# The norms' sums of squares take a PSUM slot of the bank pool instead of the aux pool

## The chip, the cores and the metric

The kernel runs on one core of a Trainium2 chip. The metric is the device time of one execution in microseconds, the median of several runs. Profiles are taken from one profiled execution; their times are counted from the start of its span. PE is TensorE, DVE is VectorE, ACT is ScalarE, and SP's queue issues most of the transfers.

## The reference

The reference is the trunk of a diffusion model over 512 latent tokens (SEQ) and 256 context tokens (CTX), with a model width of 1024. There are two layers. Each has a half-step SwiGLU, a token mixer and another half-step SwiGLU; the mixer is a bidirectional S5 state space model in layer 0 and a bidirectional gated linear attention (GLA) with four heads in layer 1. Cut to what matters here:

```python
def rmsnorm(x, w):
    xf = x.astype(F32)
    y = xf * lax.rsqrt(jnp.mean(xf * xf, axis=-1, keepdims=True) + NORM_EPS)
    return (y * w.astype(F32)).astype(x.dtype)

def ffn_half_step(x, w_norm, shift, scale, gate, w_in, w_out):
    h = rmsnorm(x, w_norm) * (1.0 + scale) + shift
    return x + 0.5 * gate * swiglu_ffn(h, w_in, w_out)

for i in range(DEPTH):
    mod_x = (jnp.einsum('bd,de->be', jax.nn.silu(c), ada_w[i]) + ada_b[i])[:, None, :]
    ...
    x = ffn_half_step(x, ...)
    hx = rmsnorm(x, norm_w[i, 1]) * (1.0 + sx[4]) + sx[3]
    # S5 in layer 0, GLA in layer 1
    x = x + sx[5] * yx
    x = ffn_half_step(x, ...)
return rmsnorm(x, final_norm_w)
```

Every step begins with an RMS norm over the width, with a shift, a scale and a gate that are products of the conditioning vector with large matrices. In the GLA each head's output goes through a norm of its own (over 256 values) before a gate and the output product.

## The kernel before

The stream `xT` is held transposed: 8 tiles of 128 channels on the partitions, 768 tokens along the free axis. So the sum of squares of a token runs over the partitions, and PE forms it. `squares` (L142) squares the 8 tiles on ACT (L147, L150) and adds them up on DVE (L151). `rstd` (L154) then multiplies each stretch of 128 tokens of that sum by a column of ones (L163), which puts the sums of 128 tokens on the partitions, in one column of a PSUM tile for each stretch. DVE L167 is the only reader of that tile. Three Newton steps on DVE (L169 to L175) make the reciprocal root `y` of it, and `spread` (L178, matmul L182) broadcasts `y` back over the partitions into a PSUM tile, which the norm's multiplications (L201) read. ACT L218 and DVE L219 split the normed operand `h` into a high and a low part.

All large products are made of three passes (`mm3`, L113 to L115): weight high times operand high, weight high times operand low, weight low times operand high. ACT L88 and DVE L89 split each weight.

PSUM has one pool with two tags of tiles of 128 partitions by 512 floats: `bank` with 6 slots (products, modulation blocks, spreads, the transposes of the start and of the end, the GLA's V tiles and outputs) and `aux` with 2 slots (the sums of L163, the columns of a modulation block at L406, small transposes, the level products, transposes and states of the GLA heads, and small steps of the S5 stage).

`rstd` is called 22 times: twice at the start (halves of the tokens), three times each for the norm ahead of S5, for the norm behind it and for the two norms between the half-steps of layers 0 and 1 and ahead of the GLA (thirds of the tokens), four times in the GLA (once a head, with two parts of 4 stretches each), twice for the norm behind the GLA, and twice at the end. In the norms the call stands in a queue of work that `tick` counts down: `norm` puts the sum some steps after the squares, and the spread three steps after the sum.

A modulation block (L399 to L406) is 16 matmuls of the conditioning vectors with a quarter of the weights into one `bank` tile; ACT L403 copies it (`adar`), four matmuls L406 bring it into columns in an `aux` tile, and DVE L446 adds the bias. At the start four such blocks follow the two sums in the program.

In the GLA the work of one head is: products of queries and keys level by level (`level`, L1210 to L1244, `aux` tiles), decays (`decays`, L1259 to L1268), transposes and states (L1287 to L1304, `aux` tiles), outputs (two `bank` tiles, matmuls L1320 to L1322, squares `gsq` on ACT L1324 and gating on DVE L1326), the gates of the next head, and then `rstd`. The squares `gsq` and the tile `geb` of decay factors (in the levels at L1231) share the two slots of one tag in SBUF. The spread of that sum and the normalised output (`normed`, which makes `goh` and `gol`) come some levels into the next head. Between these steps `fill` takes projections of the next heads (V tiles by L1109 to L1111, keys and queries by `mm3` from `h`) and output products of the head before (`goh`, `gol`) out of lists that are written by hand (`ORDER`, `COUNTS`).

At the end the last half-step SwiGLU does its last products for two halves of 256 tokens. After each half `final` scales `xT` by the norm weight (L1576), makes the squares and the sum, transposes the result in four `bank` tiles (L1583) and multiplies by `y` (L1586, L1588). So the program has the first half's products, its sum, its transposes, and only then the second half's products.

The order of instructions on each engine is not that of the program alone. The framework plans a timeline of its own, in which the program's order is the priority: work that stands later in the program is moved ahead into time that the plan shows as idle. The tiles of a tag are allocated as the program runs.

Of the kernel before, what the change touches and what calls it, by code (L numbers as in the profile page):

```python
# [38 lines left out]
class Core:  # L39
# [114 lines left out]
    def rstd(self, parts, count=D, scale=1.0):  # L154


        nc = self.nc
        n = parts[0].shape[-1]
        nt = n // P
        b = self.aux()  # L160
        for t in range(nt):
            for i, part in enumerate(parts):
                nc.tensor.matmul(b[:, t:t + 1], part[:, t * P:(t + 1) * P], self.ones[:, 0:1],  # L163
                                 start=(i == 0), stop=(i == len(parts) - 1))
        v, y, z = (self.tmp.tile([P, 4], F32, tag=f"rs{i}", name="rs", bufs=2)[:, :nt] for i in range(3))
        i32 = mybir.dt.int32
        nc.vector.tensor_scalar(out=v, in0=b[:, :nt], scalar1=1.0 / (count * scale * scale),  # L167
                                scalar2=EPS / (scale * scale), op0=ALU.mult, op1=ALU.add)
        nc.vector.tensor_scalar(out=y.bitcast(i32), in0=v.bitcast(i32), scalar1=-0.5, scalar2=1597463007.0,  # L169
                                op0=ALU.mult, op1=ALU.add)  # L170
        nc.vector.tensor_scalar(out=v, in0=v, scalar1=-0.5, scalar2=None, op0=ALU.mult)  # L171
        for _ in range(3):
            nc.vector.tensor_mul(z, y, y)  # L173
            nc.vector.tensor_mul(z, z, v)  # L174
            nc.vector.scalar_tensor_tensor(out=y, in0=z, scalar=1.5, in1=y, op0=ALU.add, op1=ALU.mult)  # L175
        return y
# [1438 lines left out]
```

## Time and profile before

| | us |
|---|---|
| median of 3 runs | 2891.98 |
| lowest and highest run | 2890.7 and 2893.82 |
| profiled execution, its own time | 2892.6 |
| its span | 2890.8 |
| PE busy | 2734.3 (95%) |
| DVE busy | 1795.5 (62%) |
| ACT busy | 856.8 (30%) |

The mean granted clock of PE in that execution was 0.967 of full speed. Rows of the timeline have the start, the duration, the engine, the line, the operation, the tile written and the tiles read, the shapes and a count where several instructions are put together; in square brackets stands the idle time of the engine before it and what ended it. Groups of lines have the count, then the busy time and the mean duration in nanoseconds. Matmuls are pipelined, so that the durations of neighbours overlap, and sums of them can be more than the time they take together.

### The profile page before, as it was taken

How to read it: one execution, taken by the hardware profiler on the slowest of the kernel's cores; microseconds unless marked ns; L12 is line 12 of the kernel's file. 1: busy time of each engine (PE TensorE's matmuls, PEld its weight loads, DVE VectorE, ACT ScalarE, POOL GpSimd, SP SyncE). 2: the span in 40 equal slices, each digit the busy share in tenths (PEclk: the TensorE clock that was granted, in tenths of full speed). 3: DMA queues.
4: the chain of work that ended last, by engine and by line, in shares of the span. 5: the costliest groups of instructions: out<-in, count | busy, mean ns of one | idle time of the engine just before them, and what ended most of it. 6: DMA issues, size and time to landing. Idle time of an engine off the chain costs nothing. (4 is left out here: it accounts for less than half of the span.)

```text
span 2890.8 us, 44937 instructions
## 1 busy us (share of the span) xinstructions
PE 2734.3 (95%) x18231; PEld 2579.4 (89%) x18231; DVE 1795.5 (62%) x4080; ACT 856.8 (30%) x1386; POOL 22.3 (1%) x57
## 2 busy tenths in 40 slices
PE   7999999996559999999999999999999899799998
PEld 5899999995459999999999999999988798688887
DVE  6699999436894565557427555665268687643433
ACT  4222222224362421122123221121236453332223
POOL 0000000000020000000000000000000000000000
PEclk9999999997779999999999999999999899899999
DMA  6545554516653133334321333333103112233330
GB/s 225 162 115 154 150 161 137 173 65 198 220 149 99 59 96 102 95 111 121 91 59 45 110 106 106 101 104 95 54 23 88 44 45 74 66 116 91 94 93 30
DMA packets 396044, 305.43 MB, mean 106 GB/s; under 512 B 57994, under 2 KB 344188, under 8 KB 395836
## 3 DMA queue, kind: packets, MB, share of 16 engines
q1 hardware_dynamic: 391228, 293.12, 34.6%
q10 hardware_dynamic: 4608, 9.44, 0.9%
q8 instruction: 143, 2.34, 0.3%
q14 instruction: 65, 0.53, 0.1%
HBM read 275.77 MB, written 30.41 MB: 106 GB/s over the span
## 5 line engine op out<-in xcount | busy, mean ns | idle before, releaser
L113 PE MATMUL bank<-h,whi 128*128 128x384 f32 (+3 forms) x3160 | 1044.0, 333 | 8.6 <-ACT whi L88 6.1
L114 PE MATMUL bank<-h,whi 128*128 128x384 f32 (+3 forms) x3160 | 1049.1, 332 | 0.2 <-DVE h L219 0.2
L115 PE MATMUL bank<-h,wlo 128*128 128x384 f32 (+3 forms) x3160 | 1046.9, 332 | 0.0
L113 PEld LDWEIGHTS bank<-h,whi 128*128 128x128 f32 (+1 forms) x3160 | 593.5, 189 | 30.3 <-ACT whi L88 6.7
L88 ACT CAST whi<-wraw 128x1024 fp32r<-128x1024 f32 x313 | 327.3, 1048 | 982.0 <-PE bank L114 930.0
L114 PEld LDWEIGHTS bank<-h,whi 128*128 128x128 f32 (+1 forms) x3160 | 595.6, 189 | 17.7 <-DVE h L219 0.5
L115 PEld LDWEIGHTS bank<-h,wlo 128*128 128x128 f32 (+1 forms) x3160 | 594.3, 188 | 17.6 <-issue 0.6
L89 DVE TENSOR_TENSOR wlo<-wraw,whi 128x1024 fp32r<-128x1024 f32 x313 | 380.5, 1219 | 243.5 <-ACT whi L88 240.0
L114 PE MATMUL bank<-ml,whi 128*128 128x384 f32 (+2 forms) x1360 | 448.0, 330 | 0.0
L113 PE MATMUL bank<-mh,whi 128*128 128x384 f32 (+2 forms) x1360 | 446.0, 331 | 2.1 <-DVE xT L279 1.2
L115 PE MATMUL bank<-mh,wlo 128*128 128x384 f32 (+2 forms) x1360 | 446.0, 329 | 0.0
L279 DVE SCALAR_TENSOR_TENSOR xT<-bank,hg,xT 128x256 f32<-128x256 f32 (+2 forms) x488 | 220.7, 499 | 198.0 <-PE bank L115 197.6
L264 DVE TENSOR_TENSOR sg<-sg,bank 128x384 f32<-128x384 f32 (+2 forms) x166 | 89.4, 539 | 352.8 <-PE bank L115 338.2
L113 PEld LDWEIGHTS bank<-mh,whi 128*128 128x128 f32 x1360 | 256.4, 189 | 9.5 <-DVE xT L279 1.5
L114 PEld LDWEIGHTS bank<-ml,whi 128*128 128x128 f32 x1360 | 257.0, 189 | 6.4 <-issue 0.4
L115 PEld LDWEIGHTS bank<-mh,wlo 128*128 128x128 f32 x1360 | 256.5, 189 | 6.3 <-issue 0.2
L427 DVE SCALAR_TENSOR_TENSOR adaacc<-wraw,cs,adaacc 128x512 f32<-128x512 f32 x336 | 236.9, 744 | 19.1 <-DMA wraw<-in_ada_w_dram 18.6
L265 ACT CAST mh<-sg 128x384 fp32r<-128x384 f32 (+2 forms) x166 | 83.5, 503 | 312.5 <-DVE sg L264 311.5
L263 ACT ACTIVATE sg<-bank 128x384 f32<-128x384 f32 (+2 forms) x166 | 79.5, 479 | 198.5 <-PE bank L115 198.4
L266 DVE TENSOR_TENSOR ml<-sg,mh 128x384 fp32r<-128x384 f32 (+2 forms) x166 | 89.7, 541 | 24.2 <-ACT mh L265 24.1
L150 ACT ACTIVATE sq<-xT 128x256 f32<-128x256 f32 (+1 forms) x126 | 52.1, 428 | 58.7 <-DVE xT L279 39.5
L201 DVE SCALAR_TENSOR_TENSOR nt<-xT,sc,bank 128x256 f32<-128x256 f32 (+2 forms) x136 | 61.6, 474 | 11.5 <-PE bank L182 8.5
(298 smaller groups left out, 2337.0 us busy)
## 6 DMA issues: line engine op xcount, KB each, us to landing
wraw<-in_ffn_w_in_dram SPq DMA_DIRECT2D x176, 512.0 KB, 4.0
wraw<-in_ada_w_dram SPq DMA_DIRECT2D x111, 512.0 KB, 3.8
wraw<-in_ffn_w_out_dram SPq DMA_DIRECT2D x88, 512.0 KB, 3.4
wraw<-in_gla_w_in_dram SPq DMA_DIRECT2D x24, 512.0 KB, 4.0
s5R<-s5r ACTq DMA_DIRECT2D x16, 512.0 KB, 2.8
s5O<-s5g SPq DMA_DIRECT2D x64, 128.0 KB, 2.7
wraw<-in_s_w_glu_dram SPq DMA_DIRECT2D x16, 512.0 KB, 6.1
big<-in_ada_w_dram SPq DMA_DIRECT2D x12, 512.0 KB, 8.8
```

The source lines that it names most:

```text
L88: nc.scalar.copy(out=hi[:, :n], in_=raw[:, :n])
L89: nc.vector.tensor_tensor(out=lo[:, :n], in0=raw[:, :n], in1=hi[:, :n].bitcast(F32), op=ALU.subtract)
L113: mm(out, wh, a[0], start=first, stop=False)
L114: mm(out, wh, a[1], start=False, stop=False)
L115: mm(out, wl, a[0], start=False, stop=last)
L201: nc.vector.scalar_tensor_tensor(out=t[:, a - s:z - s], in0=self.xT[:, k, a:z], scalar=sc[i][:, k:k + 1], in1=r[:, a - s:z - s], op0=ALU.m ...
L263: nc.scalar.activation(sg, banks[0][:, :e - s], AF.Silu)
L264: nc.vector.tensor_mul(sg, sg, banks[1][:, :e - s])
L265: nc.scalar.copy(out=mh[:, o], in_=sg)
L266: nc.vector.tensor_tensor(out=ml[:, o], in0=sg, in1=mh[:, o].bitcast(F32), op=ALU.subtract)
L279: nc.vector.scalar_tensor_tensor(out=self.xT[:, d, a:z], in0=banks[d][:, a - s:z - s], scalar=gate[i][:, d:d + 1], in1=self.xT[:, d, a:z], ...
L427: nc.vector.scalar_tensor_tensor(out=acc[:, v], in0=w[:, k], scalar=col, in1=acc[:, v], op0=ALU.mult, op1=ALU.add)
```

## The change

The PSUM tile into which `rstd` forms its sums is taken from the six slots of `bank` and not from the two slots of `aux`. The instructions and their operands stay as they are; the 22 calls all go this way.

```diff
         nc = self.nc
         n = parts[0].shape[-1]
         nt = n // P
-        b = self.aux()
+        b = self.bank()
         for t in range(nt):
             for i, part in enumerate(parts):
                 nc.tensor.matmul(b[:, t:t + 1], part[:, t * P:(t + 1) * P], self.ones[:, 0:1],
```

## The prediction

> **What bounds the kernel now.** I read first the busy times of the engines, then the windows of single stages, then the timeline around each matmul of L163.
>
> ```profile
> span 2890.8 us, 44937 instructions
> ...
> PE 2734.3 (95%) x18231; PEld 2579.4 (89%) x18231; DVE 1795.5 (62%) x4080; ACT 856.8 (30%) x1386; POOL 22.3 (1%) x57
> ```
>
> ```profile
> 2250.00:2270.00 20.00, 12.30 (x57) 10.95 (x58) 19.88 (x60) 6.91 (x11) 0.10 (x1) 0.61 0.00 1
> 2270.00:2369.75 99.75, 99.75 (x597) 86.70 (x596) 71.44 (x147) 46.16 (x79) 0.51 (x3) 0.99 0.23 64
> 2530.00:2865.00 335.00, 335.00 (x1587) 277.03 (x1586) 130.63 (x157) 88.00 (x115) 0.00 (x0) 1.00 0.29 85
> ```
>
> The columns of a window are its length, then the busy time of PE, weight load, DVE, ACT and POOL, the granted clock, the DMA share and GB/s. PE is the bound, and in the long product stages it is never idle. An idle microsecond that the change makes ahead of such a stage is lost, one that it closes is won. Only the short stages between (here GLA head 0, where DVE is busy for 19.88 of 20 us) can hide anything.
>
> **The change part by part.** No instruction is added or removed: 140 matmuls of L163 write, and 22 instructions of L167 read, a slot of another tag.
>
> ```profile
> L163 PE MATMUL aux<-ones,ssq x76: 164/250/353, 30.0 to 2881.1; 128*128 128x1 f32 x76
> ...
> L167 DVE TENSOR_SCALAR rs<-aux x22: 146/152/163, 31.0 to 2881.4; 128x2 f32<-128x2 f32 x16, 128x4 f32<-128x4 f32 x4, 128x3 f32<-128x3 f32 x2
> ```
>
> So all of the cost is in the order. I take it that the slots of one tag are given out in program order, while the planner moves other work far ahead. Three places speak for it:
>
> ```profile
> 2212.84 0.58 ACT L403 COPY adar<-bank 128x512 f32<-128x512 f32 x1
> ...
> 2241.80 0.28 PE L163 MATMUL aux<-ones,gsq 128*128 128x1 f32 x2
> ...
> 2241.95 1.03 PE L406 MATMUL aux<-quarter,adar 128*128 128x2 f32 x8
> ...
> 2255.36 2.05 PE L1242 MATMUL aux<-gqc,gkc 128*128 128x128 f32 x8 [2.98 <-DVE gqc L1239]
> ...
> 2269.99 1.71 PE L182 MATMUL bank<-ident,rs 128*128 128x128 f32 x8
> ...
> 2271.45 0.36 PE L1109 MATMUL bank<-whi,h 128*128 128x256 f32 x1
> ```
>
> The input of L406 was ready at 2213.42, but its aux tile stands behind that of the sum in the program, and it ran directly after the sum's first matmul, 28.5 us later. In the same way V tile 5 (L1109) ran directly after the spread (L182) whose bank slot stands ahead of it, though PE stood idle for 2.98 us before. The third place is the start, below. With a bank slot, every later product that the planner has hoisted past a sum must wait for that sum's first matmul, and so for its squares; later aux tiles no longer do.
>
> *Start.* The second half's sum holds back the modulation blocks (L399):
>
> ```profile
> 22.50:34.70 12.20, 8.73 (x52) 1.84 (x52) 1.00 1.05 386
> ```
> ```profile
> 33.88 0.56 DVE L151 TENSOR_TENSOR ssq<-ssq,sq 128x384 f32<-128x384 f32 x1
> 34.73 0.83 PE L163 MATMUL aux<-ones,ssq 128*128 128x1 f32 x6
> ...
> 35.42 1.66 PE L406 MATMUL aux<-quarter,adar 128*128 128x2 f32 x8
> ...
> 47.04 0.16 DVE L446 TENSOR_TENSOR mod<-aux,cols 128x8 f32<-128x8 f32 x1
> ```
> ```profile
> 36.00:49.00 13.00, 13.00 (x48) 7.97 (x47) 6.89 (x23) 5.17 (x7) 0.00 (x0) 0.50 0.87 231
> ```
>
> 52 matmuls of L399, 8.73 us, lie before the second sum, and some 12 groups of four have to follow it. The sum itself cannot come before 34.44, where DVE ends. In exchange L406 and the block copies no longer wait. Before, the last shift came at 47.04 on a PE of half clock. After: 34.7, 12 groups of 0.43 us (full clock, 8.73/52 less overlap) to 0.85 us, and three turns through L406 of 1.0 to 1.7 us give 42.9 to 50.0. That is -4 to +3; I take +0.5, near the middle.
> The trace shows that a PE which was idle is granted 0.50. The Trainium skill (TensorE: Matmul & The Clock Gate, Part 1: The HAM clock gate) says that the array works at half clock until about 3.4 us of activity, so that blocks that now start after a wait would start slow; by that alone this term would be an estimated +2 in place of +0.5. The trace agrees as far as its 0.50 goes, but shows 13 us of it rather than 3.4.
>
> *Norms of the FFN halves and the S5 stage.*
>
> ```profile
> 1558.59 0.98 PE L163 MATMUL aux<-ones,ssq 128*128 128x1 f32 x4 [2.34 <-DVE ssq L151]
> ...
> 2126.61 0.58 PE L163 MATMUL aux<-ones,ssq 128*128 128x1 f32 x4 [2.48 <-DVE ssq L151]
> ```
> ```profile
> 670.00:675.00 5.00, 0.99 (x89) 0.77 (x75) 2.62 (x11) 3.59 (x7) 0.00 (x0) 0.89 0.96 295
> ```
>
> These two sums lie in idle gaps of PE and would move into busy PE or delay it: 0.5 us each (0.98 and 0.58 busy), +1.0 (0 to +2). The sums before the S5 stage move by some product groups, but there PE is busy for 0.99 of 5 us and DMA for 0.96: covered, 0; without that cover it would be the 0.6 us of a sum.
>
> *GLA head 0.* The V projection of head 1 was hoisted ahead of head 0's sum:
>
> ```profile
> L1109 PE MATMUL bank<-whi,h 128*128 128x256 f32 x32 | 9.8, 307 | 0.0
> ...
> L1302 PE MATMUL aux<-gv,gkt 128*128 128x256 f32 x8 | 2.8, 442 | 0.0
> L1296 PE MATMUL aux<-gv,gkt 128*128 128x256 f32 x4 | 1.0, 378 | 0.0
> L1287 PE MATMUL aux<-ident,gkb 128*128 128x128 f32 x5 | 0.9, 272 | 0.0
> ```
> ```profile
> 2237.00:2250.00 13.00, 11.37 (x100) 11.09 (x98) 5.73 (x18) 4.35 (x10) 0.00 (x0) 1.00 0.01 1
> ```
> ```profile
> 2247.12 0.43 DVE L1231 TENSOR_TENSOR geb<-gcb 128x256 f32<-128x256 f32 x1 [2.61 <-PE aux L163]
> ```
>
> The lines are those of 2222.5 to 2237.2; L1110 and L1111 have 32 each too. 14.7 us less 4.7 of the other three leaves 10.0 us of moved products. They now start after the sum. Transposes, states and outputs no longer share PE with them and end earlier, by some 5 to 8 us (half to most of the 10). With them the sum comes earlier, and so does geb, which waited 2.61 us for it and starts the levels of head 1. The moved products then fill the idle time of the levels: 1.63 us (2237 to 2250) and 7.70 (2250 to 2270), 9.3 in all. I reckon an idle 3.1 before the sum (10.0 less a chain 6.9 shorter) and 4.5 left in the levels, 7.6: -2. Ends: all of the wait stays (+3 when the levels' gaps take 7 of the 10), or the sum moves by the full 8 (-5).
>
> *Heads 1 to 3.*
>
> ```profile
> L113 PE MATMUL bank<-goh,whi 128*128 128x512 f32 x16 | 6.5, 407 | 0.0
> ...
> L113 PE MATMUL bank<-h,whi 128*128 128x384 f32 x16 | 5.6, 353 | 0.0
> ...
> L1174 PE MATMUL bank<-glow,gwg 32*128 32x384 f32 x1 | 0.5, 481 | 0.0
> ```
> ```profile
> 2369.75:2392.50 22.75, 22.75 (x114) 20.20 (x114) 18.94 (x39) 13.72 (x25) 0.00 (x0) 1.00 0.10 27
> ```
> ```profile
> 2241.58 0.39 PE L1322 MATMUL bank<-gqb,xT 128*128 128x128 f32 x2
> ...
> 2398.41 0.28 PE L163 MATMUL aux<-ones,gsq 128*128 128x1 f32 x2
> ```
>
> Head 2 is the worst place: K of head 3 and the output product of head 1 (16 matmuls each in L113, L114 and L115, 96 of the window's 114) lay ahead of its sum. The other 18 have some 4.6 us, so 18.2 us are moved. The chain of head 2 before its sum (transposes, states, outputs) then has PE to itself. If PE alone paced it, the sum would come 18.2 us earlier, at 2380.2. From 2369.75 to there PE has the 4.6 us and some 3 of outputs (24 matmuls like the L1322 pair, by 0.39 a pair at most 4.7, and pairs overlap), so 10.4 less 7.6, some 3 us idle, of which the planner may fill a part with work that stands earlier in the program: +2.5 (0 to +11; the upper end where the chain doesn't speed up). All that follows is full PE, so it is lost. Head 1's sum has next to nothing hoisted past it, and nothing stands behind head 3's: 0 and 0; without that it would be head 2's price again.
>
> *End of GLA.*
>
> ```profile
> 2501.37 0.99 PE L163 MATMUL aux<-ones,ssq 128*128 128x1 f32 x4 [11.63 <-DVE rs L173]
> ```
>
> This sum ran after 11.63 us of idle PE directly ahead of the spread. The planner may place it elsewhere: -0.4 (-1 to +2).
>
> *Final norm.*
>
> ```profile
> 2865.00 1.47 PE L1583 MATMUL bank<-ident,fy 128*128 128x128 f32 x12
> ...
> 2866.23 0.36 PE L113 MATMUL bank<-mh,whi 128*128 128x256 f32 x1
> ...
> 2866.91 0.42 DVE L151 TENSOR_TENSOR ssq<-ssq,sq 128x256 f32<-128x256 f32 x1 [0.28 <-ACT sq L150]
> ...
> 2869.62 0.50 PE L163 MATMUL aux<-ones,ssq 128*128 128x1 f32 x4
> ```
> ```profile
> 2880.74 0.62 PE aux L163 x4
> ```
>
> The first half's squares end at 2867.33. Until now transposes (L1583) and the second half's products filled PE meanwhile, and L163 came at 2869.62. All of them stand behind that sum in the program; now PE is idle from 2865.0 to about 2867.4: +2.2 (1.5 to 3). In the tail the last transposes come after the sum at 2880.74 and run beside the Newton steps on DVE: 0 (at most +0.3).
>
> **Sum:** 0.5 + 1.0 - 2 + 2.5 - 0.4 + 2.2 = +3.8. The profiled execution took 2892.6 us (its span 2890.8 and 1.8 around it), 0.6 over the median 2892.0. 2892.6 + 3.8 = 2896.4; less 0.6, 2895.8.
>
> **The rivals.** *Slower: head 2 waits.* One mechanism: the transposes and states of head 2 are paced by DVE (18.94 busy of 22.75 us) and not by PE, so the chain hardly speeds up and up to 18.2 us of products have nothing ahead of them. It decides once the first sum comes after about 2386: from there idle grows one for one, to +11 by 2389. With 8 to 11 in place of 2.5: 2901 to 2904. For it speaks the busy DVE; against it that much of that DVE work is weight splitting and gates of head 3 that can stand back.
> *Faster: head 0 closes.* All of the 10 us fit into the 9.3 us of gaps and the levels start 8 us earlier: -8 in place of -2, 2889.8, and with the start at its low end (-4) 2885. Against it: DVE is busy for 19.88 of 20 us in those levels, so they can't get shorter, only earlier.
> *The slots aren't given out in program order* but to whoever comes first in the plan. Then nothing is blocked, and six slots are enough: 2892.0. The three places above speak against it.
>
> **How the numbers follow.** About 0.2%, 5.8 us, is what a measurement of this kernel can tell from no change: under 2886.2 is faster, over 2897.8 slower. The likeliest case (chance 0.52, own range 2889 to 2900) puts 0.15 of its chance over 2897.8, 0.34 within and 0.03 below, since the planner lays the whole order anew and the ends of the terms add to some 6 us each way. Head 2 waits: 0.21, all slower. Head 0 closes: 0.15, 0.12 of it faster. No order: 0.12, all within. Together faster 0.15, within 0.49, slower 0.36. The range runs from 2886.5, the faster case, to 2905, the end of the slower one.
>
> **What would show it.** In the profile after: the first L163 of head 2 before about 2383 with L113 goh behind it (right), or later than 2386 (the slower rival); V tiles of head 1 behind the first L163 of head 0, and geb no longer waiting for it; L399 of the start after the second sum; an idle PE of about 2.2 us near 2865 ended by DVE L151. Products that stand behind a sum in the program and still run ahead of it would refute the rule of order, and with it the whole working; so would a changed busy time of PE.

## The result, and the profile after

The changed kernel takes 2917.86 us (2917.47 to 2918.34 in 4 runs), the kernel before beside it 2891.34 (2889.96 to 2893.82). The ratio is 1.0092, with a 95% interval of 1.0081 to 1.0104: 26.5 us slower. Forecast were 2895.8 us, in a range of 2886.5 to 2905, with "no change" as the likeliest outcome. The time lies 13 us beyond the range, on the side of the slower rival.

First the head of the page of the profile after.

```profile
span 2915.7 us, 44943 instructions
...
PE 2742.7 (94%) x18231; PEld 2585.3 (89%) x18231; DVE 1799.0 (62%) x4080; ACT 859.5 (29%) x1386; POOL 22.3 (1%) x57
```

The span is 24.9 us longer. The same 18231 matmuls kept PE busy for 8.4 us more (2742.7 against 2734.3), so they were slower; the other 16.5 us are idle time. For the place I take the same instruction in both traces and subtract its start before from its start after. This lag is flat for hundreds of microseconds in the product stages and steps up at a few places:

| stretch (time before) | growth of the lag, us | forecast, us |
|---|---|---|
| start, to 650 | +3.3 | +0.5 |
| S5 stage, to 970 | -4.0 | 0 |
| norm behind the S5 stage, 970 to 1020 | +4.6 | not priced |
| norm ahead of layer 1, 1555 to 1600 | +1.6 | +0.5 |
| norm ahead of the GLA, to 2123 | 0.0 | +0.5 |
| GLA and the norm behind it, 2123 to 2505 | +15.8 | +0.1 |
| into the last half-step, to 2860 | +0.4 | 0 |
| last norm and tail | +3.2 | +2.2 |

The first two rows cancel, and are not to be read as an effect: in runs whose code is that of the kernel before up to 970 us, the lag there lay between -6.0 and +1.3 us. So what is left is the GLA, the norm behind the S5 stage, the end, and a smaller step at the norm ahead of layer 1.

For the GLA, windows between the same events (the last sum ahead of it and the first product of the half-step behind it), the kernel before first. After the length come the busy time of PE, the granted clock, the DMA share and GB/s.

```profile
2123.08:2504.53 381.45, 346.70 (x2194) 0.93 0.23 64
```
```profile
2128.55:2525.84 397.29, 354.38 (x2191) 0.91 0.20 59
```

It is 15.8 us longer: 8.2 us more idle PE (42.9 against 34.7) and 7.7 us more busy time for the same work, at a lower clock. In these windows PE was busy for 47.4 us at a granted clock of 0.50, against 32.5 before. So half of the loss there is not a wait but matmuls at half clock in and behind the waits.

The timeline of PE ahead of head 1's sum, before and after the change:

```profile
2310.64 0.34 PE L113 MATMUL bank<-h,whi 128*128 128x384 f32 x1
2310.81 0.38 PE L1322 MATMUL bank<-gqb,xT 128*128 128x128 f32 x2
```
```profile
2308.66 0.70 PE L1302 MATMUL aux<-gv,gkt 128*128 128x256 f32 x2 [0.33 <-ACT xT L1298]
2311.16 0.97 PE L1302 MATMUL aux<-gv,gkt 128*128 128x256 f32 x2 [1.80 <-DVE xT L1304]
2316.05 0.80 PE L1322 MATMUL bank<-gqb,xT 128*128 128x128 f32 x2 [3.92 <-DVE xT L1304]
2316.64 0.64 PE L1320 MATMUL bank<-gs,gv 128*128 128x128 f32 x2
...
2323.07 0.39 PE L1322 MATMUL bank<-gqb,xT 128*128 128x128 f32 x2
2323.30 0.28 PE L163 MATMUL bank<-ones,gsq 128*128 128x1 f32 x2
```

Before, 25 products of `h` (2306.36 to 2310.64) stand between the last state matmuls and the outputs, and PE doesn't wait. After, 24 such products have run already, from 2302.57 to 2308.66, ahead of the last states; the next ones start right behind the L163 (2323.30). So nothing is left between these rows: PE waits for DVE's state updates (L1304), and the output matmuls then take 0.64 us a pair, later 0.39. At head 2 no product at all runs between 2371.66 and the sum; these rows are the end of it:

```profile
2393.38 0.80 PE L1322 MATMUL bank<-gqb,xT 128*128 128x128 f32 x2 [3.67 <-DVE xT L1304]
...
2399.56 0.28 PE L163 MATMUL bank<-ones,gsq 128*128 128x1 f32 x2
```

What DVE did meanwhile is in its own timeline after the change:

```profile
2310.63 0.47 DVE L1304 SCALAR_TENSOR_TENSOR xT<-xT,gtot,aux 128x256 f32<-128x256 f32 x1
2311.02 0.42 DVE L1194 TENSOR_TENSOR_SCAN gcb<-glg,gz 128x128 f32<-128x128 f32 x1
2311.36 0.67 DVE L1194 TENSOR_TENSOR_SCAN gxc<-glg,gz 128x256 f32<-128x256 f32 x1
...
2313.99 1.05 DVE L1194 TENSOR_TENSOR_SCAN gcb<-glg,gz 128x128 f32<-128x128 f32 x3
2314.96 1.04 DVE L1304 SCALAR_TENSOR_TENSOR xT<-xT,gtot,aux 128x256 f32<-128x256 f32 x2
```

Between two state updates of head 1 it works through the scans (L1194) of the gates of head 2, and from 2311.94 to 2313.99 through what these set free in head 2's first levels and decays. This order is the plan's; `gates` of the next head are called ahead of the sum in the program.

The norm behind the S5 stage. Before, PE never waited here; after, the second third's spread comes late:

```profile
993.40 0.50 PE L163 MATMUL bank<-ones,ssq 128*128 128x1 f32 x4
...
1002.87 0.68 PE L182 MATMUL bank<-ident,rs 128*128 128x128 f32 x4 [3.11 <-DVE rs L175]
```
```profile
982.69 0.50 PE L163 MATMUL aux<-ones,ssq 128*128 128x1 f32 x4
...
999.22 0.60 PE L182 MATMUL bank<-ident,rs 128*128 128x128 f32 x4
```

The sum itself (second fence: before) moved by 10.7 us. From it to the spread stand the Newton steps, which DVE fits in among its other work in 8.8 us, and the spread waits for the last of them. Behind the wait the granted clock is 0.50 from 1004.2 to 1007.6 us, so that 3.11 us of idle time cost 4.6.

The end has an idle PE ahead of either sum, as forecast for the first, ended by DVE L151:

```profile
2889.08 0.61 PE L163 MATMUL bank<-ones,ssq 128*128 128x1 f32 x4 [2.23 <-DVE ssq L151]
...
2905.23 0.92 PE L163 MATMUL bank<-ones,ssq 128*128 128x1 f32 x4 [2.23 <-DVE ssq L151]
2906.00 3.29 PE L1583 MATMUL bank<-ident,fy 128*128 128x128 f32 x16
```
```profile
2878.70 1.91 PE L1583 MATMUL bank<-ident,fy 128*128 128x128 f32 x16
2880.74 0.61 PE L163 MATMUL aux<-ones,ssq 128*128 128x1 f32 x4
```

In the tail the 16 transposes moved from ahead of the sum (second fence: before) to behind it, and take 3.29 us where they took 1.91; the granted clock is 0.50 from 2905.4 to 2908.8 us.

### The profile page after: what moved, and what is told of

Its sections match the earlier page's. It is cut to its first block, busy times and chain, and to the rows that moved or that the text cites. A ratio compares the mean times of both kernels' runs of the same rounds, so it can differ in the third digit from the quotient of the medians.

```text
span 2915.7 us, 44943 instructions
## 1 busy us (share of the span) xinstructions
PE 2742.7 (94%) x18231; PEld 2585.3 (89%) x18231; DVE 1799.0 (62%) x4080; ACT 859.5 (29%) x1386; POOL 22.3 (1%) x57
## 5 line engine op out<-in xcount | busy, mean ns | idle before, releaser
L113 PE MATMUL bank<-h,whi 128*128 128x384 f32 (+3 forms) x3160 | 1042.4, 333 | 15.5 <-ACT h L218 9.4
L114 PE MATMUL bank<-h,whi 128*128 128x384 f32 (+2 forms) x3160 | 1048.0, 333 | 0.3 <-DVE h L219 0.3
L115 PE MATMUL bank<-h,wlo 128*128 128x384 f32 (+2 forms) x3160 | 1045.7, 332 | 0.0
L113 PEld LDWEIGHTS bank<-h,whi 128*128 128x128 f32 (+1 forms) x3160 | 593.1, 189 | 37.1 <-ACT h L218 10.3
L114 PEld LDWEIGHTS bank<-h,whi 128*128 128x128 f32 x3160 | 595.6, 189 | 17.9 <-DVE h L219 0.6
L115 PEld LDWEIGHTS bank<-h,wlo 128*128 128x128 f32 x3160 | 594.3, 188 | 17.7 <-issue 0.6
L201 DVE SCALAR_TENSOR_TENSOR nt<-xT,sc,bank 128x256 f32<-128x256 f32 (+2 forms) x136 | 62.3, 477 | 20.5 <-PE bank L182 16.6
```

The lines of the kernel that those rows point to most:

```text
L113: mm(out, wh, a[0], start=first, stop=False)
L114: mm(out, wh, a[1], start=False, stop=False)
L115: mm(out, wl, a[0], start=False, stop=last)
L201: nc.vector.scalar_tensor_tensor(out=t[:, a - s:z - s], in0=self.xT[:, k, a:z], scalar=sc[i][:, k:k + 1], in1=r[:, a - s:z - s], op0=ALU.m ...
```

## The experiments

In most of the kernels `rstd` counts its calls and takes a bank slot for some of them only:

```diff
     def rstd(self, parts, count=D, scale=1.0):
+        self.nr = getattr(self, 'nr', -1) + 1
...
-        b = self.bank()
+        b = self.bank() if self.nr in (14, 15, 16, 17) else self.aux()
```

Calls 0 and 1 are the start, 2 to 4 the norm ahead of S5, 5 to 7 the norm behind it, 8 to 13 the two norms between the half-steps and ahead of the GLA, 14 to 17 the GLA heads, 18 and 19 the norm behind the GLA, 20 and 21 the last norm. "Growth in the GLA" is the lag at 2600 less the lag at 2000 us of time before, taken as above; it is 16.2 us in the changed kernel, and lies between -0.2 and +0.1 in three runs that leave this stretch as it was.

### The heads' sums alone

> Only the four sums of the GLA heads take a bank slot; the other 18 stay in aux. Theory of order (products that stand behind a sum in the program wait for it): the GLA's part of the loss alone. In the changed kernel the lag behind the kernel before grows from 5.8 us at the start of the GLA to 21.7 behind it, so +15.9 us, about 2907, with PE idle ahead of the outputs of heads 1 and 2. Rival (the bank pool is a slot short): heads take few products at a time, so under +5, and no idle time ahead of the sums.

Calls 14 to 17 in bank. 2907.5 us, ratio 1.0057 (1.0042 to 1.0072). The growth in the GLA is 17.5 us, and all else stays. PE idles for 1.79 and 3.96 us ahead of the outputs of head 1, and 1.20 and 3.67 ahead of those of head 2. The theory of order named the time to within a microsecond, from the lag that the changed kernel had shown there.

### All but the heads

> The other 18 sums take a bank slot and the four of the GLA heads stay in aux. Theory of order: what is left of the loss, 26.5 - 15.9 = +10.6 us, about 2902, if the stages add up: start +3.3, S5 stage -4.0, second norm behind S5 +4.6, norm ahead of layer 1 +1.6, end of the GLA -1, final norm +2.4 in each of its two halves. Rival (slot short): most of the +26, since nearly all products lie outside the GLA.

2896.72 us, ratio 1.0019 (1.0009 to 1.0028): +5.2 where +10.6 was expected. The steps at 970 (+4.6) and 1555 (+1.4) and at the end are there, but the stretch from 2000 to 2600 gains 4.0 us, through the norm behind the GLA. The parts do not add up there: that gain is 1.1 us when the norm is changed alone (below).

### A tag of their own for the sums

```diff
-        b = self.bank()
+        b = self.ps.tile([P, 512], F32, tag="sums", name="sums", bufs=1)
...
-        return self.ps.tile([P, 512], F32, tag="bank", name=name, bufs=6)
+        return self.ps.tile([P, 512], F32, tag="bank", name=name, bufs=5)
```

> The sums take a PSUM slot of a tag of their own (one slot), and the bank pool has five slots in place of six. Nothing but the sums themselves stands in that tag's order. Theory of order: no product waits for a sum, and no aux tile either, so within 5 us of the kernel before (2886 to 2897). Rival (slot short): the products have five slots at every moment, at least as bad as the changed kernel, 2918 or more.

2894.86 us, ratio 1.0013 (1.0003 to 1.0022). With five slots for the products at every moment the kernel loses 3.4 us, not 26 (2.1 of it in the GLA; what they are is not shown). So it is not that the bank pool is short of a slot; it is whose turn the slot is.

### Head 0 alone

> Only the sum of GLA head 0 takes a bank slot. Theory of order: there the moved V products fill the idle time of the levels of head 1. Up to 2270 us the changed kernel has 3.5 us less idle PE than before in this stage and some 4 us less of work at half clock, so -7.5 us, about 2884. Rival (every sum in bank costs): +3 to +5.

2893.53 us, ratio 1.0008 (0.9999 to 1.0017); growth in the GLA +3.1. A miss by 10 us. The V products of head 1 do fill the levels of head 1's first part, and the idle time there (9.3 us before) is gone. But PE now waits 5.7 us ahead of head 0's sum (2.81, 1.37 and 1.52 us), and another 5.7 us come up a head later, in the timeline of PE from 2330 us on, where the kernel before has none:

```profile
2330.15 1.13 PE L1242 MATMUL aux<-gqc,gkc 128*128 128x128 f32 x8 [0.83 <-DVE gqc L1240]
2335.53 3.75 PE L1242 MATMUL aux<-gqc,gkc 128*128 128x128 f32 x16 [4.25 <-DVE gqc L1240]
2339.89 1.44 PE L182 MATMUL bank<-ident,rs 128*128 128x128 f32 x5 [0.60 <-DVE rs L175]
```

The work that filled those levels had been drawn forward. A gap that is closed with work from a later stage opens there, and an idle-time balance of one stage is no gain.

### Head 2 alone, heads 1 and 2

> Only the sum of GLA head 2 takes a bank slot. With heads 1 and 2 in bank the lag grew by 14.0 us within the GLA, and no idle PE lay at head 1, so all of it should be head 2's: +12 to +14, about 2905, with 7 to 8 us of idle PE ahead of the outputs of head 2. If heads 1 and 2 share it: +6 to +8.

2904.94 us, ratio 1.0046 (1.0029 to 1.0063), growth in the GLA +13.9.

> Only the sums of GLA heads 1 and 2 take a bank slot. Theory (each blocked head costs its own idle PE and the half clock behind it, about 9 us at head 1 and 13.7 at head 2, and head 0 gained some 7.6 of it back): +22 within the GLA, about 2913. Rival (what head 0 seems to gain is only moved): the 17.5 of all heads less the 3.1 of head 0 alone, +14, about 2906. If neither chain is held by anything but PE: +3.

2904.18 us, ratio 1.0044 (1.0029 to 1.0059), growth +14.0. So head 1's sum in bank adds nothing to head 2's, which has nearly all of it. (In the changed kernel head 1 waits too, and that takes the order of both heads. With head 0 in aux, as here, 24 products of `h` run between head 1's last states and its outputs, and there is no wait. With head 0 in bank and head 1 in aux, as in the run of head 0 alone, those 24 run earlier, but 47 more are drawn ahead of head 1's outputs in their place. With both in bank these 47 stand behind head 1's sum.) The windows of head 2 alone, from the states to the outputs and through the outputs:

```profile
2362.00:2377.40 15.40, 7.61 (x25) 3.81 (x23) 11.19 (x27) 11.04 (x22) 0.00 (x0) 0.68 0.04 11
2377.40:2384.00 6.60, 6.60 (x43) 6.60 (x44) 0.75 (x1) 0.64 (x2) 0.00 (x0) 0.71 0.00 0
```

PE is busy for half of the first window, at a clock of 0.68, and the second, though PE is busy throughout, has 0.71. The idle 7.8 us are a little over half of the 13.9.

### The sums of heads 0 to 2 called later

```diff
-            y = c.rstd(H[h]["sqs"], DV, 0.5)
+            if h == HEADS - 1:
+                y = c.rstd(H[h]["sqs"], DV, 0.5)
...
+                if h and e == 0:
+                    y = c.rstd(H[h - 1]["sqs"], DV, 0.5)
                 if h and e == NORMED:
```

> As the run with the four heads' sums in bank, but the sums of heads 0 to 2 are called later in the program: in the next head, behind its demanded keys and queries and its first level. Theory of order: keys, queries and output products then stand ahead of the sum and are no longer held by it; only the V products behind it are. Within the GLA the growth of the lag falls from 17.5 us to -3 to +5, about 2890 to 2897, with no idle PE ahead of the outputs of heads 1 and 2. Rival (the bank slot itself, or the chain of states with its load on DVE): the idle time ahead of the outputs stays, +12 or more.

2905.46 us, ratio 1.0047 (1.0032 to 1.0062), growth +14.4. Half a hit: no gap of over 0.6 us is left ahead of the outputs of heads 1 and 2, as the theory of order has it. But the time doesn't come back. The idle time is now in the levels of the next heads. The V products that could fill them have run before, 24 of them ahead of the later sum and the last at 2334, and the next ones come only behind the spread (L182):

```profile
2337.36 1.13 PE L1242 MATMUL aux<-gqc,gkc 128*128 128x128 f32 x8 [0.82 <-DVE gqc L1240]
2342.74 3.75 PE L1242 MATMUL aux<-gqc,gkc 128*128 128x128 f32 x16 [4.25 <-DVE gqc L1240]
2347.10 2.08 PE L182 MATMUL bank<-ident,rs 128*128 128x128 f32 x8 [0.60 <-DVE rs L175]
```

### The gates behind the sum

```diff
-            if h < HEADS - 1:
-                step(lambda h: gates(h + 1))
             y = c.rstd(H[h]["sqs"], DV, 0.5)
+            if h < HEADS - 1:
+                step(lambda h: gates(h + 1))
```

> As the run with the four heads' sums in bank, but the gates of the next head are called behind the sum in place of ahead of it. Theory (ahead of the outputs of heads 1 and 2 PE waits for DVE, which works through the gates' scans, L1194 and L1188, before the last state updates, L1304): the idle time ahead of the outputs, 5.8 and 6 us, falls to under 2 each, and the outputs come some 5 us earlier; the gates then come later and may cost the same again ahead of the next head's decays. So the place of the idle time is what tells, the time itself 2895 to 2912. Rival (the chain is paced by its own round trips between PE, ACT and DVE): the gaps stay at 5 to 6 us.

The call of the gates is followed by its own portion of `fill`, which moves with it: 24 products at head 1, none at heads 0 and 2. With the heads' sums in bank as in the first experiment, this takes 2892.09 us, ratio 1.0001 (0.9991 to 1.0010); growth in the GLA 2.1 in place of 17.5. The time is better than the forecast span. Ahead of the outputs of heads 1 and 2 PE waits 0.57 us, and DVE has no scan between the state updates. Timelines of DVE and PE at head 1, and then the first experiment's row there:

```profile
2292.65 0.48 DVE L1304 SCALAR_TENSOR_TENSOR xT<-xT,gtot,aux 128x256 f32<-128x256 f32 x1 [1.25 <-PE aux L1302]
2293.31 1.09 DVE L1304 SCALAR_TENSOR_TENSOR xT<-xT,gtot,aux 128x256 f32<-128x256 f32 x2 [0.18 <-PE aux L1302]
2307.39 0.42 DVE L1194 TENSOR_TENSOR_SCAN gcf<-glg,gz 128x128 f32<-128x128 f32 x1
```
```profile
2294.46 0.49 PE L1322 MATMUL bank<-gqb,xT 128*128 128x128 f32 x2 [0.57 <-DVE xT L1304]
...
2299.03 0.28 PE L163 MATMUL bank<-ones,gsq 128*128 128x1 f32 x2
```
```profile
2306.24 0.79 PE L1322 MATMUL bank<-gqb,xT 128*128 128x128 f32 x2 [3.96 <-DVE xT L1304]
```

The outputs come at 2294.46 in place of 2306.24 in the first experiment, and the products that wait for the sum start with it; they then cover the late gates. At head 2, where the gates alone moved, the wait ahead of the outputs falls from 3.67 to 0.57 us. The chain was held by the gates on DVE, and not by its own round trips.

### The gates behind the sum, all sums in aux

> All sums in aux as in the kernel before, with the gates of the next head called behind the sum. If the gates ahead of the state updates cost only where no product may fill PE meanwhile (the bank slot's doing), this alone changes little: within 4 us of the kernel before. If the gates' place is worth the same with either slot, it gains some 12 to 15 us: about 2878.

2891.65 us, ratio 1.0001 (0.9992 to 1.0011). By itself the gates' place is worth nothing: there the products fill PE while DVE is at the gates. It costs only together with the bank slot.

### The norm behind the S5 stage

> Only the three sums of the norm behind the S5 stage (the calls at 977 to 1012 us) take a bank slot. Theory: the second third's sum stands behind more product tiles and comes some 10 us later; its Newton steps on a full DVE take another 9 us, so the spread, and PE with it, waits: the lag behind the kernel before grows by 4.6 us between 970 and 1020 us, and the whole is about +4.6, 2896. Rival (a sum costs only its own 0.5 us on PE): under +1 in that stretch.

Calls 5 to 7 in bank: 2894.78 us, ratio 1.0014 (1.0004 to 1.0024): +2.5 where +4.6 was expected. The lag does grow by 4.6 us between 970 and 1020, and falls by 0.9 at the norm ahead of layer 1, whose code is as before. The spread waits:

```profile
990.68 0.50 PE L163 MATMUL bank<-ones,ssq 128*128 128x1 f32 x4
1000.15 0.68 PE L182 MATMUL bank<-ident,rs 128*128 128x128 f32 x4 [3.12 <-DVE rs L175]
```

Then the sum alone called earlier, the spread in its place:

```diff
-            s5.glu(yp, halves, thirds, norm(0, 2, 12))
+            s5.glu(yp, halves, thirds, norm(0, 2, 6, 9))
```

> As the run with only these three sums in bank, but each sum is called 6 steps after the squares in place of 12 and its spread 9 steps later in place of 3, so that the spread keeps its place in the program and only the sum moves ahead. Theory (the lateness of the sum is what costs): the second sum comes near 985, its Newton steps end ahead of the spread, and the growth of the lag between 970 and 1020 us is gone: 0 to +1. Rival (it is the bank slot, or the load of DVE): +4 to +5 stays.

2892.11 us, ratio 0.9998 (0.9989 to 1.0008); the growth is 0.5 us, and PE doesn't wait:

```profile
984.16 0.50 PE L163 MATMUL bank<-ones,ssq 128*128 128x1 f32 x4
998.85 0.60 PE L182 MATMUL bank<-ident,rs 128*128 128x128 f32 x4
```

From sum to spread there are 14.7 us now, where there were 9.5. The same slot, the same DVE; only the lateness went, and the loss with it.

### The norm behind the GLA, and the last norm

> Only the two sums of the norm behind the GLA take a bank slot. Where 18 sums in bank left out the heads, the lag fell by 4.8 us between 2400 and 2530 us; in the changed kernel by 0.9. Theory (the bank slot frees the modulation block's aux tile and the order there): -4.8 us in this stretch, about 2887. Rival (the Newton steps there stand on DVE behind weight splits that wait for the transfers, so that the stage ends when the weights land): 0, whatever the slot.

2890.01 us, ratio 0.9992 (0.9983 to 1.0002); growth -1.1. Between the two expectations, and no difference that can be told. The spread there waited 7.15 us for the Newton steps against 11.63 before, but two other waits came up.

> Only the two sums of the last norm take a bank slot. Theory: the first half's transposes and the second half's products stand behind the first sum; PE is idle for 2.2 us from the end of the first half's products to the sum, and the time rises by 2.4, about 2894. In the tail nothing: the transposes run beside the Newton steps.

2896.14 us, ratio 1.0017 (1.0008 to 1.0027): +4.6, twice the forecast. The idle 2.23 us are there ahead of each sum. What was not foreseen: the transposes behind the sum are slow (2.83 us in the first half and 3.45 in the second, against 1.91), and in the second half they outlast the Newton steps, so that the chain of waits ends on them. The granted clock was 0.50 from 2869.5 to 2872.9 us and again from 2886.6 to 2890.0. In the changed kernel it stayed at 1.00 behind the first of these waits: the same 2.23 us of idle time cost 4.0 us by the lag here, and 2.4 there.

### Both causes taken away, and a try for more

The changed kernel with all sums in bank, the gates behind the sums and the sums behind the S5 stage earlier (the two diffs above):

> The changed kernel with all 22 sums in bank, and two moves in the program: the gates behind the sums, and the sums of the norm behind the S5 stage earlier. If the two causes are what costs there, the heads' +16 to +17.5 and the norm's +4.1 go: 2917.9 - 16 - 4 = about 2898, with the rest in the last norm, the norms ahead of layer 1 and the start. If they only move the idle time elsewhere: 2908 or more.

2894.85 us, ratio 1.0012 (1.0002 to 1.0021). Of 26.5 us, 23 are gone with two moves in the program and no change to a slot; growth in the GLA -1.6. What stays, +3, is about what the last norm has.

> The sums of the heads and of the norm behind the GLA in bank, the gates behind the sums, the rest in aux: the places where bank was no worse. Adding what was measured apart (heads with the gates moved 0.0 to +0.6, norm behind the GLA -1.5) it gives about 2891, not to be told from the kernel before; under 2886 it would beat it.

Calls 14 to 19 in bank, gates behind the sums: 2892.16 us, ratio 1.0004 (0.9995 to 1.0013). No kernel of this study beats the one before by more than the noise.

## Why the prediction was wrong

**The rule of order** held. At the places looked at, the products that stand behind a sum in the program came behind it: the modulation blocks at the start behind both sums, V, key and output products behind the heads' sums, the last products behind the first half's sum. The tag of its own shows that the order, not the number of slots, does it. The rival "not in program order" is out.

**The sum of the terms** is where it failed, at three terms and for one shared reason: a term was priced by PE's work, while what decides is how long the chain from the squares to the spread, or from the states to the sum, takes on DVE (in head 0's run the waits ahead of the sum and those that come back later are ended, but for one on ACT, by DVE).

*GLA head 2* (+2.5 forecast, +13.9 alone). The step that failed: "If PE alone paced it, the sum would come 18.2 us earlier, at 2380.2". It came 8 us earlier only: at 2383.75 in the run of head 2 alone, which had a lag of -6.4 ahead of it, so at 2390.1 on the time of the kernel before, against 2398.41. DVE paced it, with the next head's gates between the state updates. The slower rival named this mechanism, with 0.21 of the chances and up to +11, and its sign held too, a first sum "after about 2386". Against it the prediction set that the gates of head 3 "can stand back"; in the plan they didn't, and once they were called behind the sum the growth in the GLA fell from 17.5 to 2.1 us. What the rival lacked is the clock: idle time ahead of the outputs was priced once, and is paid nearly twice, since the states and outputs around it run at half clock. In the changed kernel the GLA has 8.2 us more idle time and 7.7 us of slower work.

*GLA heads 0 and 1* (-2 and 0 forecast). Head 0 alone costs +3.1, and head 1 adds nothing to head 2. The step "The moved products then fill the idle time of the levels" was right for head 0 and didn't pay: PE waits 5.7 us ahead of the sum where 3.1 was reckoned, and the products were missing a head later, for another 5.7. Nor did the sum come "earlier, by some 5 to 8 us": it came 1.0 us earlier (2238.86 in the run of head 0 alone, 2240.8 with the lag of -1.9 taken out, against 2241.80). And `geb` still waits for it, against the sign that the prediction named; DVE in the changed kernel:

```profile
2250.71 0.43 DVE L1231 TENSOR_TENSOR geb<-gcb 128x256 f32<-128x256 f32 x1 [2.94 <-PE bank L163]
```

Together with head 2 it all comes to 16 or 17.5, so the heads aren't independent terms at all: the filling of one is taken from the next.

*The norm behind the S5 stage* (not in the sum; +4.6). The prediction's part on norms names two sums that lay in gaps, and passes over the one that lay in full products. That one moved by 10.7 us, and the 0.5 us that a sum costs on PE were taken for the price, where the path is sum, 8.8 us of Newton steps, spread. The norm ahead of layer 1 (+1.6 against +0.5) is the same step, smaller: its last sum moved from the gap at 1558.59 to 1577.81, into full products, and its spread waits for DVE too:

```profile
1584.37 0.68 PE L182 MATMUL bank<-ident,rs 128*128 128x128 f32 x4 [1.25 <-DVE rs L175]
```

*Start and S5.* The order changed as described, and more so: the first sum also holds the blocks back. PE is idle for 9.65 us there. The low end of that term also used 0.43 us for a group of four matmuls, "8.73/52 less overlap", where four times 8.73/52 gives 0.67. But the S5 stage behind it takes it up, and between runs with the same code this stretch differs by more than the term, so neither +0.5 nor +3.3 is shown.

*Final norm* (+2.2; lag +2.4 in the first half). The mechanism and the idle 2.2 us were right; that they cost no more was luck of the clock, since in the run of the last norm alone the same wait cost 4.0. That the last transposes "run beside the Newton steps on DVE: 0" was not right: behind an idle stretch and at a granted clock of 0.50 they took 3.29 us in place of 1.91 and ended last, +0.8.

*The test that the prediction set itself* was also wrong at one point: "a changed busy time of PE" was to refute the working. It changed by 8.4 us with the same matmuls, and refutes nothing of the order; it is the clock: PE was busy at a granted 0.50 for 122.5 us after and 104.3 before, and half of the difference is 9.1.

On the clock, the rows show that a pair of outputs took 0.64 us until 2321.3 and 0.39 from 2321.7, 5.7 us after the outputs had begun; at head 2 it was 3.5 us (2393.38 to 2396.88).
The Trainium skill (TensorE: Matmul & The Clock Gate, Part 1: The HAM clock gate) gives about 3.4 us of sustained activity to come back to full clock, by windows that run freely. Head 2 agrees with it; head 1 took longer. By the granted clock of the trace the stretches at 0.50 were 10.2 us long at head 1 (2311.5 to 2321.7) and 20.5 us at head 2 (2376.3 to 2396.8), three and six times 3.4. Counted in such steps, head 2's outputs began with a step (2393.4) and head 1's in the middle of one (2314.9 to 2318.3), and the clock rose one full step after, which would explain the difference.

## What to carry to other kernels

Where a planner hands out the slots of a tag in program order, the choice of a tag is a choice of what must wait for what: before moving a tile to another pool, list what stands behind it in the program and runs ahead of it today, and what fills PE if that can't. Price such a move by the latency of the chain on the engine that paces it, from the last input to the next use, and not by the instruction's own time. An idle stretch in a dense PE stage costs more than its length where the clock falls with it: in the GLA 8.2 us of idle time came with 7.7 us of slower matmuls, while 2.23 us in the last norm cost 2.4 us where the clock stayed up. And filling that one stage draws from the next is no gain.

## What the runs showed of the hardware

The clock also fell without a gap. At head 2 of the changed kernel the trace has no idle PE from 2369.75 to 2379.00 us, and the granted clock goes from 1.00 to 0.50 at 2376.3, 4.6 us after the last of the large products (2371.66). Behind it PE was busy for 8.38 of 14.40 us, in pieces with waits of 0.56 to 3.67 us between them, and the clock was 0.50 throughout:

```profile
2369.75:2376.30 6.55, 6.55 (x26) 4.22 (x25) 3.45 (x5) 3.42 (x7) 0.00 (x0) 1.00 0.34 108
2376.30:2379.00 2.70, 2.70 (x8) 1.60 (x7) 0.48 (x1) 0.40 (x1) 0.00 (x0) 0.50 0.29 86
2379.00:2393.40 14.40, 8.38 (x19) 4.27 (x18) 10.70 (x26) 10.95 (x21) 0.00 (x0) 0.50 0.00 1
2393.40:2400.00 6.60, 6.60 (x44) 6.60 (x45) 0.75 (x1) 0.84 (x2) 0.00 (x0) 0.74 0.00 0
```

So this stage of small dependent matmuls ran its own chain at half clock, and handed a slow start to the dense work behind it. That products of another head, run in between, keep the clock up is what the kernel before shows at the same place, where the window from 2369.75 to 2392.50 has a clock of 1.00.
